# Attention output layer: weight blocks split a block sooner, and the next stage's first two blocks held behind the turned probabilities of heads 5 and 6

## The chip, the cores and the metric

The kernel runs on one core of one Trainium2 chip. The metric is the device time of one execution in microseconds (us), as a median over runs. The kernel before takes 922.94 us (three runs, 922.83 to 923.55). A profiled execution gives the trace from which every time below is read.

## What is computed

A two-layer encoder trunk over 256 rows of 1024 values. Each layer is half a SwiGLU feed-forward, a mixer, and half a SwiGLU feed-forward; the mixer of the first layer is a convolution, that of the second is attention with compressed queries, keys and values. The change touches that attention and the start of the feed-forward behind it:

```
def mla(h, positions, w_a, g_q, g_kv, w_uq, w_ukv, w_o):
    ...
    for blk in range(seq // Q_BLOCK):
        ...
        s = (q_nope . k_nope + q_rope . k_rope) * scale
        s = jnp.where(mask, s, -inf)
        p = softmax(s)
        outs.append(p @ v)
    return concatenate(outs).reshape(seq, N_HEADS * V_HEAD) @ w_o
...
h = h + mla(...)
h = h + 0.5 * swiglu_ffn(rmsnorm(h, ffn_norm2[i]), ...)
```

There are 8 heads, 256 query rows in two blocks of 128, and head widths of 128 (plain), 64 (rotary) and 128 (values).

## The kernel before

**Weights.** All weights stream from HBM in blocks of 128 x 2048 fp32 (1 MB), in one fixed list. `load` (L153) sends a block through three steps: SyncE starts a transfer into a `raw` buffer, ScalarE rounds it into `hi` (L171, two casts of 128 x 1024), VectorE forms the rest `lo = raw - hi` (L175, two subtractions). Four `raw` and four `hi`/`lo` buffers rotate, so a transfer waits for the `lo` of four blocks earlier, and a cast waits until TensorE has read the block four places earlier. A product with weights is three matmuls (`mm3`, L281): `lo` by the high part of the data, `hi` by the high part, `hi` by the low part (L284, L287, L288).

**How far ahead.** `weights(n, more, ahead)` takes the next block of the list and, through `load_ahead`, issues loads for blocks that lie up to `ahead` places on; the default is 2 blocks, `W_BUFS - 1` is 3 and `W_BUFS` is 4. The casts and subtractions are written into the program where `load` is called. A scheduler then orders each engine's instructions; `@urgent` code (softmax, row sums, splits of the data) gets a higher priority, and `behind` keeps weight splits after the last few urgent instructions of the same engine.

**Attention (`mla_in`, L1076).** The last blocks of the list there are, in order, `wuq[2]`, `wuq[0]`, `wukv[0]` (keys), `wukv[1]` (values), `wuq[1]` (queries of heads 4 to 7), and four blocks `wo0` to `wo3` of the output layer. Behind them come `f0`, `f1`, ... of the last feed-forward. For each head: `scores` (L1192) makes the scores `sc` on TensorE, 12 matmuls; `softmax` takes row maxima on VectorE (`nm`, L1209 and L1210), exponentials on ScalarE (`pr`, L1212), and scales them on VectorE (L1214, L1216). `probs` (L1219) turns the probabilities on TensorE (`tp`, three matmuls on L327) and copies them back on ScalarE (`ptT`, L1222). `values` (L1225) multiplies with the values (`pv`, L1227 and L1228), and rounds the result on ScalarE (`Oh`, L1229) with its rest on VectorE (`Ol`, L1230). `Rows` is the output layer: a block of `wo` serves two heads, and each head gives 12 matmuls into `o`.

**The loop (L1239).** Step `i` takes the scores of head `i`, turns head `i-2`, and multiplies head `i-3`; at `i` of 6 and 8 `o.block` adds two heads to the output, and `o.finish` does the last four and goes over to the feed-forward. PSUM has 4 banks for `o` and other products, 3 shared by `sc` and `tp`, and 1 for `pv`; a score tile can only begin when the exponentials that read the bank before it are done.

Of the kernel before, what the change touches and what calls it, by code (L numbers as in the profile page):

```python
# [19 lines left out]
P = 128  # L20
# [19 lines left out]
W_BUFS = 4  # L40
# [47 lines left out]
def trunk(ctx: ExitStack, tc: tile.TileContext, x, xt, pos, invf, gains, gfin, wdw,  # L88
          f1w13, f1w2, f2w13, f2w2, cw1, cw2, wa, wuq, wukv, wo, out):
    nc = tc.nc  # L90
# [12 lines left out]
    def uid(s):  # L103
        n_uid[0] += 1
        return f"{s}_{n_uid[0]}"
# [4 lines left out]
    def bank(tag, name):  # L110
        return ps.tile([P, 512], F32, tag=tag, name=uid(name), bufs=BANKS[tag])
# [30 lines left out]
    def order(ins, first):  # L142
        tc.add_manual_dep(ins.ins, first.name, mybir.DependencyInfo(
            mybir.DependencyClass.NoSync, mybir.DependencyReason.DATA), reason="order")

    def behind(ins):

        for first in ahead_of.get(ins.ins.engine, [])[-BEHIND:]:
            order(ins, first)

    low_later = []

    def load(src, pieces=1):  # L153
        if isinstance(src, tuple) and src[0] == "fast":
            return load_fast(src[1])
        if isinstance(src, tuple):
            raw = rawp.tile([P, HB], F32, tag="raw", name=uid("raw"))
            nc.sync.dma_start(raw, src[1])
            return raw
        later = len(loaded) in (conv_block[-1], conv_block[-2])  # L160
        n = src.shape[-1]
        raw = rawp.tile([P, HB], F32, tag="raw", name=uid("raw"))
        hi = wp.tile([P, HB], F32R, tag="hi", name=uid("hi"))
        lo = wp.tile([P, HB], F32R, tag="lo", name=uid("lo"))
        if len(loaded) < 7:
            fetch(raw[:, :n], src)
        else:
            nc.sync.dma_start(raw[:, :n], src)
        for i in range(pieces):
            c = slice(i * n // pieces, (i + 1) * n // pieces)  # L170
            behind(nc.scalar.copy(hi[:, c], raw[:, c]))  # L171
            if later:
                low_later.append((lo[:, c], raw[:, c], hi[:, c].bitcast(F32)))
            else:
                behind(nc.vector.tensor_sub(lo[:, c], raw[:, c], hi[:, c].bitcast(F32)))  # L175
        return hi, lo

    def load_fast(src):

        raw = rawp.tile([P, HB], F32, tag="raw", name=uid("raw"))  # L180
        sums = rawp.tile([P, HB], F32, tag="raw", name=uid("sums"))
        nc.sync.dma_start(raw, src)
        v = raw.rearrange("p (b n) -> p b n", n=512)
        t = sums.rearrange("p (b n) -> p b n", n=512)
        behind(nc.gpsimd.tensor_tensor(t[:, 0:2, :], v[:, 0:4:3, :], v[:, 1:2, :].to_broadcast([P, 2, 512]), op=ALU.add))  # L185
        behind(nc.vector.tensor_add(t[:, 2, :], t[:, 0, :], v[:, 3, :]))
        behind(nc.vector.tensor_add(t[:, 3, :], t[:, 2, :], v[:, 2, :]))
        out = []
        for x, cols in ((raw, ((0, 512), (1024, 2048))), (sums, ((0, 1024), (1024, 2048)))):
            hi = wp.tile([P, HB], F32R, tag="hi", name=uid("hi"))  # L190
            lo = wp.tile([P, HB], F32R, tag="lo", name=uid("lo"))
            for c0, c1 in cols:
                behind(nc.scalar.copy(hi[:, c0:c1], x[:, c0:c1]))  # L193
                behind(nc.vector.tensor_sub(lo[:, c0:c1], x[:, c0:c1], hi[:, c0:c1].bitcast(F32)))  # L194
            out.append((hi, lo))
        return out
# [14 lines left out]
    def slots(b):  # L211
        return 2 if isinstance(blocks[b], tuple) and blocks[b][0] == "fast" else 1

    def load_ahead(ahead=W_BUFS - 2):
        b = n_used[0]
        while b < len(blocks) and slots(b) <= ahead:
            ahead -= slots(b)
            b += 1
        load_to(b)

    def load_to(last):
        while len(loaded) < last:
            loaded.append(load(blocks[len(loaded)], PIECES))

    def weights(n=1, more=True, ahead=W_BUFS - 2):
        out = []
        for _ in range(n):
            n_used[0] += 1
            if more:
                load_ahead(ahead)  # L230
            else:
                load_ahead(0)
            out.append(loaded[n_used[0] - 1])
        return out
# [12 lines left out]
    def fetch(to, src):  # L247

        dma = nc.sync.dma_start(to, src)
        if first_dma:  # L250
            order(dma, first_dma[-1].ins)
        first_dma.append(dma)

    fetch(xk[:, :1], xt[:, :1])
    for k in range(KT):
        c = slice(k % 4 * 512, k % 4 * 512 + 512)
# [67 lines left out]
    def transposed(src, q, n, after=(), turned=None):  # L324
        b = bank("B", "tp")
        for j in range(n):
            tp = nc.tensor.transpose(b[:, j * P:(j + 1) * P], src[:, (q + j) * P:(q + j + 1) * P], ident)  # L327
            if turned is not None:
                turned.append(tp)
            for a in after:  # L330
                order(tp, a.ins)
        return b
# [743 lines left out]
    def mla_in(act, X, make_next, cc, sn):  # L1076
# [65 lines left out]
        def nope(part, dst, nk, ch, cl, width, h0, heads):  # L1142

            hi, lo = part
            for i in range(heads[0], heads[1], 2):
                b = bank("A", "nope")
                for e in range(2):
                    for k in range(nk):
                        c = slice(k * width + (i + e) * P, k * width + (i + e + 1) * P)
                        mm3(b[:, e * S:(e + 1) * S], hi[:, c], lo[:, c], ch[:, k, :], cl[:, k, :],  # L1150
                            k == 0, k == nk - 1)
                nc.scalar.copy(dst[:, h0 + i:h0 + i + 2, :], b.rearrange("p (e t) -> p e t", t=S))
# [15 lines left out]
        part, = weights()  # L1168
        nope(part, QN, 4, CQh, CQl, 512, 0, (0, 4))
        for t in range(NT):  # L1170
            b = transposed(kd[t], 0, 1)
# [3 lines left out]
        for tb in range(NT):  # L1175
            b = transposed(qr[tb], 0, 4)
            nc.scalar.copy(QR[:, :, tbs(tb)], b.rearrange("p (j t) -> p j t", t=P))
        kpart, = weights()
        nope(kpart, KN, 2, CKh, CKl, D, 0, (0, H))
        (hi, lo), = weights()  # L1180
        for tb in range(NT):
            for d in range(2):
                b = bank("A", "v")
                for k in range(2):
                    c = slice(k * D + d * 512, k * D + d * 512 + 512)
# [6 lines left out]
        def scores(hd):  # L1192
            b = bank("B", "sc")
            sc = {0: b[:, :P], 1: b[:, P:P + S]}
            for qb in range(NT):
                n = (qb + 1) * P
                nc.tensor.matmul(sc[qb], QN[:, hd, tbs(qb)], KN[:, hd, :n], start=True, stop=False)
                nc.tensor.matmul(sc[qb], QR[:, hd // 2, tbs(qb)], KR[:, hd % 2, :n], start=False, stop=False)
                nc.tensor.matmul(sc[qb][:, n - CHUNK:n], mq, mk, start=False, stop=True)
            return softmax(sc)  # L1200
# [18 lines left out]
        def probs(pr):  # L1219
            b = transposed(pr, 0, 3)  # L1220
            pt = act.tile([P, 3 * P], F32, tag="ptT", name=uid("ptT"), bufs=2)
            nc.scalar.copy(pt, b[:, :3 * P])  # L1222
            return pt

        def values(hd, pt):  # L1225
            b = bank("C", "pv")
            nc.tensor.matmul(b[:, :S], VV[:, 0, hd * VH:(hd + 1) * VH], pt[:, :S], start=True, stop=False)  # L1227
            nc.tensor.matmul(b[:, P:S], VV[:, 1, hd * VH:(hd + 1) * VH], pt[:, S:], start=False, stop=True)  # L1228
            nc.scalar.copy(Oh[:, hd, :], b[:, :S])  # L1229
            nc.vector.tensor_sub(Ol[:, hd, :], b[:, :S], Oh[:, hd, :].bitcast(F32))  # L1230

        pr, pt = {}, {}
        pr[0] = scores(0)
        part, = weights()
        nope(part, QN, 4, CQh, CQl, 512, 4, (0, 2))
        pr[1] = scores(1)
        nope(part, QN, 4, CQh, CQl, 512, 4, (2, 4))
        o = Rows(Oh, Ol, H)
        for i in range(2, H + 3):  # L1239
            if i < H:  # L1240
                pr[i] = scores(i)
            if i - 2 < H:
                pt[i - 2] = probs(pr[i - 2])
            if i - 3 in pt:
                values(i - 3, pt[i - 3])
            if i in (6, 8):
                o.block((i - 6) // 2)
        return o.finish(make_next, act)


# [107 lines left out]
def build(shapes):  # L1358
    import concourse.bacc as _bacc

    nc = _bacc.Bacc("TRN2", target_bir_lowering=False, num_devices=1, dynamic_dma_scratch_size=1024)
    args = [nc.dram_tensor(f"in_{n}", s, mybir.dt.from_np(np.dtype(d)), kind="ExternalInput").ap()
            for n, s, d in shapes]
    out = nc.dram_tensor("out", (S, D), F32, kind="ExternalOutput").ap()
    with tile.TileContext(nc, schedule_with_timeline_sim=True) as tc:
        trunk(tc, *args, out)
    return nc
# [9 lines left out]
```

## Time and profile before

| | |
|---|---|
| median of the runs | 922.94 us (922.83 to 923.55) |
| the profiled execution | 923.62 us, of which the span of the trace is 921.8 us |
| TensorE matmul (PE) busy | 909.6 us |
| VectorE (DVE) busy | 680.9 us |
| ScalarE (ACT) busy | 539.7 us |
| GpSimd (POOL) busy | 226.4 us |
| granted TensorE clock | 0.999 |
| the heads' part of attention | about 684 to 734 us from the span's start |

Rows of the timeline read: start, duration, engine, line, operation, out<-in, shapes, count of merged instructions, and in brackets the idle time before and who ended it. Start to start is what one instruction costs its engine; a matmul's duration includes a drain that overlaps the next one.

### The profile page before, as it was taken

Reading aid. Unit: us, or ns where it says so; the run is one execution under the profiler, and the core shown is the slowest. Engines: PE = TensorE matmul, PEld = TensorE weight load, DVE = VectorE, ACT = ScalarE, POOL = GpSimd, SP = SyncE. Lnnn points to the kernel's source line nnn. Section 1 sums busy time; section 2 is a strip of 40 time slices with the busy share of each in tenths; the row PEclk is TensorE's granted clock in tenths of the full one; section 3 lists DMA queues with packets and bytes.
Section 4 is the critical chain, followed back from the end, with each engine's and each line's share of the span. In section 5 each row is a group of like instructions: output and inputs, shape, how many; then the busy total and the mean of one; then the engine's idle time right before and its main releaser. Section 6 shows DMA issues by size and latency. Waiting matters only on the chain.

```text
span 921.8 us, 12383 instructions
## 1 busy us (share of the span) xinstructions
PE 909.6 (99%) x4293; PEld 755.5 (82%) x4293; DVE 680.9 (74%) x1052; ACT 539.7 (59%) x940; POOL 226.4 (25%) x337
## 2 busy tenths in 40 slices
PE   9999999999999999999999999999999999999997
PEld 6888888898958888888888888888998788888886
DVE  5776877689977666777976667978667476667876
ACT  6964556568877455455474544655666475444643
POOL 1101232379941100232300003224200000013223
PEclk9999999999999999999999999999999999999999
DMA  9976656653307676556756775656441557774651
GB/s 342 350 276 226 203 180 222 240 183 138 138 22 283 244 255 240 189 161 228 299 205 238 252 244 153 228 209 214 183 183 60 186 202 251 246 239 150 219 183 47
DMA packets 60399, 191.58 MB, mean 208 GB/s; under 512 B 11184, under 2 KB 33328, under 8 KB 40752
## 3 DMA queue, kind: packets, MB, share of 16 engines
q1 hardware_dynamic: 59760, 190.09, 58.9%
q8 instruction: 34, 0.56, 0.2%
q10 hardware_dynamic: 576, 0.69, 0.2%
q14 instruction: 29, 0.24, 0.1%
HBM read 178.17 MB, written 12.58 MB: 207 GB/s over the span
## 4 chain that ended last, share of the span: by engine, by line
PE 72%; DVE 8%; DMA 8%; ACT 4%; issue 3%; POOL 3%; SPq 1%; POOLq 0%; ACTq 0%; DVEq 0%
PE u L288 15%; PE u L287 15%; PE u L284 15%; DVE lo L175 5%; PE o L284 3%; PE o L287 3%; PE o L288 3%; PE gate L738 3%; DMA raw<-in_f2w 3%; DMA raw<-in_f1w 3%; PE u L738 3%; POOL sums L185 3%; PE o L978 2%; ACT hi L171 1%; DVE lo L194 1%
## 5 line engine op out<-in xcount | busy, mean ns | idle before, releaser
L175 DVE TENSOR_TENSOR lo<-raw,hi 128x1024 fp32r<-128x1024 f32 (+1 forms) x246 | 296.3, 1240 | 74.4 <-ACT hi L171 74.1
L171 ACT CAST hi<-raw 128x1024 fp32r<-128x1024 f32 (+1 forms) x250 | 247.9, 1046 | 147.7 <-PE u L288 107.9
L288 PE MATMUL u<-hi,Xl 128*128 128x512 f32 x688 | 267.8, 390 | 0.7 <-DVE Xl L345 0.7
L284 PE MATMUL u<-lo,Xh 128*128 128x512 f32 x688 | 268.1, 390 | 0.1
L287 PE MATMUL u<-hi,Xh 128*128 128x512 f32 x688 | 267.7, 389 | 0.0
L288 PEld LDWEIGHTS u<-hi,Xl 128*128 128x128 f32 x688 | 129.1, 188 | 28.2 <-DVE Xl L345 1.6
L284 PEld LDWEIGHTS u<-lo,Xh 128*128 128x128 f32 x688 | 129.2, 188 | 27.3 <-DVE lo L175 0.5
L287 PEld LDWEIGHTS u<-hi,Xh 128*128 128x128 f32 x688 | 129.2, 188 | 26.6
L185 POOL TENSOR_TENSOR sums<-raw 128x1024 f32<-128x1024 f32 x20 | 54.2, 2710 | 162.4 <-DMA raw<-in_f2w 52.7
L284 PE MATMUL o<-lo,Gh 128*128 128x512 f32 (+1 forms) x236 | 91.5, 388 | 0.7 <-DVE lo L175 0.7
L287 PE MATMUL o<-hi,Gh 128*128 128x512 f32 (+1 forms) x236 | 91.0, 386 | 0.0
L288 PE MATMUL o<-hi,Gl 128*128 128x512 f32 (+1 forms) x236 | 91.0, 386 | 0.0
L632 POOL TENSOR_TENSOR sx<-gb 128x128 f32<-128x128 f32 x20 | 10.2, 509 | 316.7 <-DMA gb<-gd 316.7
L624 ACT CAST Gh<-gb 128x512 fp32r<-128x512 f32 (+2 forms) x48 | 25.8, 539 | 63.6 <-DMA gb<-gd 63.5
L193 ACT CAST hi<-sums 128x1024 fp32r<-128x1024 f32 x40 | 41.2, 1052 | 30.7 <-PE u L288 14.7
L786 DVE SCALAR_TENSOR_TENSOR acc<-V,dw,acc 128x128 f32<-128x128 f32 (+1 forms) x174 | 57.8, 411 | 0.0
L625 DVE TENSOR_TENSOR Gl<-gb,Gh 128x512 fp32r<-128x512 f32 (+2 forms) x48 | 33.2, 705 | 31.2 <-ACT Gh L624 31.1
L194 DVE TENSOR_TENSOR lo<-sums,hi 128x1024 fp32r<-128x1024 f32 x40 | 56.1, 1432 | 0.0
L284 PEld LDWEIGHTS o<-lo,Gh 128*128 128x128 f32 x236 | 44.3, 188 | 11.0 <-DVE lo L175 2.3
L288 PEld LDWEIGHTS o<-hi,Gl 128*128 128x128 f32 x236 | 44.3, 188 | 8.9
L287 PEld LDWEIGHTS o<-hi,Gh 128*128 128x128 f32 x236 | 44.3, 188 | 8.8
L814 ACT ACTIVATE prod<-V,dw 128x128 f32<-128x128 f32 (+1 forms) x129 | 48.0, 418 | 2.8 <-POOL Y L815 1.4
(247 smaller groups left out, 1325.7 us busy)
## 6 DMA issues: line engine op xcount, KB each, us to landing
raw<-in_f2w SPq DMA_DIRECT2D x66, 1024.0 KB, 4.8
raw<-in_f1w SPq DMA_DIRECT2D x64, 1024.0 KB, 5.0
raw<-in_cw SPq DMA_DIRECT2D x12, 1024.0 KB, 5.2
gd<-gt SPq DMA_DIRECT2D x160, 64.0 KB, 2.7
gb<-gd SPq DMA_DIRECT2D x40, 256.0 KB, 3.4
raw<-in_wo SPq DMA_DIRECT2D x4, 1024.0 KB, 4.8
raw<-in_wuq SPq DMA_DIRECT2D x3, 1024.0 KB, 4.8
raw<-in_f1w SPq DMA_DIRECT2D x8, 256.0 KB, 6.2
```

Of the source, the lines that this page charges most:

```text
L171: behind(nc.scalar.copy(hi[:, c], raw[:, c]))
L175: behind(nc.vector.tensor_sub(lo[:, c], raw[:, c], hi[:, c].bitcast(F32)))
L185: behind(nc.gpsimd.tensor_tensor(t[:, 0:2, :], v[:, 0:4:3, :], v[:, 1:2, :].to_broadcast([P, 2, 512]), op=ALU.add))
L193: behind(nc.scalar.copy(hi[:, c0:c1], x[:, c0:c1]))
L194: behind(nc.vector.tensor_sub(lo[:, c0:c1], x[:, c0:c1], hi[:, c0:c1].bitcast(F32)))
L284: mm = nc.tensor.matmul(o, ah, bl, start=start, stop=False)
L287: nc.tensor.matmul(o, ah, bh, start=False, stop=False)
L288: return nc.tensor.matmul(o, al, bh, start=False, stop=stop)
L625: nc.vector.tensor_sub(dl, x, dh.bitcast(F32))
L738: mm = nc.tensor.matmul(u[:, t], w[:, c], X.x[:, k, t], start=(k == 0), stop=(k == KT - 1))
L786: ins = nc.vector.scalar_tensor_tensor(out if j == j1 - 1 else y, v, w, y, op0=ALU.mult, op1=ALU.add)
L814: prod = nc.scalar.activation(p, v, AF.Copy, scale=w)
```

## The change

The blocks of the output layer are taken one place further ahead (3 instead of 2 at two places, 4 at step `i` = 4), so that `wo0` to `wo3` are all issued before the loop's fourth step. The first two blocks of the feed-forward, `f0` and `f1`, are issued at `i` of 7 and 8, with each cast ordered behind the copy of the turned probabilities of that step (heads 5 and 6). `probs` returns that copy as well.

```
+    split_behind = []
...
-            behind(nc.scalar.copy(hi[:, c], raw[:, c]))
+            high = nc.scalar.copy(hi[:, c], raw[:, c])
+            behind(high)
+            for first in split_behind:
+                order(high, first.ins)
...
-        (hi, lo), = weights()
+        (hi, lo), = weights(1, True, W_BUFS - 1)
...
-            nc.scalar.copy(pt, b[:, :3 * P])
-            return pt
+            return pt, nc.scalar.copy(pt, b[:, :3 * P])
...
-        part, = weights()
+        part, = weights(1, True, W_BUFS - 1)
...
         for i in range(2, H + 3):
+            if i == 4:
+                load_ahead(W_BUFS)
...
-                pt[i - 2] = probs(pr[i - 2])
+                pt[i - 2], last = probs(pr[i - 2])
...
+            if i in (7, 8):
+                split_behind.append(last)
+                load_ahead(W_BUFS)
+                split_behind.clear()
```

No instruction is added or removed on any engine; SyncE and GpSimd keep their order. Line numbers after the change are 2 to 5 higher. Three places show what moves.

**ScalarE, the copies of keys and values before the heads.** `hi_1060` is `wo1`, `KN` the keys (the last copy is that of heads 6 and 7), `VV` the values. Before:

```order
L1152 COPY KN_6043<-nope_1053_6210 128x512
L1152 COPY KN_6043<-nope_1054_6224 128x512
L1152 COPY KN_6043<-nope_1055_6238 128x512
L1187 COPY VV_6045<-v_1059_6260 128x512
L1187 COPY VV_6045<-v_1060_6268 128x512
```

After:

```order
L1157 COPY KN_6043<-nope_1053_6210 128x512
L1157 COPY KN_6043<-nope_1054_6224 128x512
L173 CAST hi_1060_6261<-raw_1059_6260 128x1024 x2
L1157 COPY KN_6043<-nope_1055_6238 128x512
L1192 COPY VV_6045<-v_1062_6268 128x512
L1192 COPY VV_6045<-v_1063_6276 128x512
```

The two casts of `wo1` now stand ahead of the last copy of the keys; the casts of `wo2` take the place, behind the exponentials of head 0, where those of `wo1` stood.

**ScalarE, among the heads.** Before, from the exponentials of head 6 (`pr_1110`) to those of head 7 (`pr_1123`); `hi_1115` and `hi_1118` are `wo2` and `wo3`, `pv_1106` is head 2, `ptT_1112` head 4:

```order
L1212 ACTIVATE pr_1110_6514,sm_1109_6513<-sc_1107_6505,nm_1108_6512 128x256
L171 CAST hi_1115_6535<-raw_1114_6534 128x1024 x2
L171 CAST hi_1118_6543<-raw_1117_6542 128x1024 x2
L1229 CAST Oh_6292<-pv_1106_6500 128x256
L1222 COPY ptT_1112_6527<-tp_1111_6523 128x384
L1212 ACTIVATE pr_1123_6583,sm_1122_6582<-sc_1120_6574,nm_1121_6581 128x128
```

After, the same stretch from head 6 (`pr_1116`) to head 7 (`pr_1123`), with `Oh` of head 2 and `ptT` of head 4:

```order
L1217 ACTIVATE pr_1116_6530,sm_1115_6529<-sc_1113_6521,nm_1114_6528 128x128
L1217 ACTIVATE pr_1116_6530,sm_1115_6529<-sc_1113_6521,nm_1114_6528 128x256
L1233 CAST Oh_6300<-pv_1112_6516 128x256
L1227 COPY ptT_1118_6543<-tp_1117_6539 128x384
L1217 ACTIVATE pr_1123_6583,sm_1122_6582<-sc_1120_6574,nm_1121_6581 128x128
```

No cast of weights is left in it. Those of `wo3` (`hi_1097`) are found after, some ten rows earlier, behind the exponentials of head 3 (`pr_1092`) and ahead of `ptT` of head 2 and the exponentials of head 4 (`pr_1102`):

```order
L1217 ACTIVATE pr_1092_6435,sm_1091_6434<-sc_1089_6426,nm_1090_6433 128x256
L173 CAST hi_1097_6456<-raw_1096_6455 128x1024 x2
L1227 COPY ptT_1104_6485<-tp_1103_6481 128x384
L1217 ACTIVATE pr_1102_6472,sm_1101_6471<-sc_1099_6463,nm_1100_6470 128x128
L1217 ACTIVATE pr_1102_6472,sm_1101_6471<-sc_1099_6463,nm_1100_6470 128x256
L1233 CAST Oh_6300<-pv_1105_6487 128x256
```

So the four casts in one row behind head 6 are gone from there, and two of them stand behind head 3. The casts of `f0` go from behind the exponentials of head 7 to behind `ptT` of head 5; those of `f1` stay behind `ptT` of head 6.

**VectorE, heads 0 to 2.** Before (`nm_1064`, `nm_1072`, `nm_1081` are heads 0, 1, 2; `lo_1069` is `wo1`):

```order
L1209 TENSOR_REDUCE nm_1072_6353<-sc_1071_6346 128x1 x2
L1214 RECIPROCAL sm_1065_6302<-sm_1065_6302 128x2
L1210 TENSOR_SCALAR nm_1072_6353<-nm_1072_6353 128x2
L1216 TENSOR_SCALAR pr_1066_6303<-pr_1066_6303,sm_1065_6302 128x128
L1216 TENSOR_SCALAR pr_1066_6303<-pr_1066_6303,sm_1065_6302 128x256
L175 TENSOR_TENSOR lo_1069_6314<-raw_1067_6312,hi_1068_6313 128x1024 x2
L1214 RECIPROCAL sm_1073_6354<-sm_1073_6354 128x2
```

After (`nm_1067`, `nm_1075` are heads 0 and 1; `lo_1072` is `wo2`):

```order
L1219 RECIPROCAL sm_1068_6310<-sm_1068_6310 128x2
L1214 TENSOR_REDUCE nm_1075_6361<-sc_1074_6354 128x1 x2
L1221 TENSOR_SCALAR pr_1069_6311<-pr_1069_6311,sm_1068_6310 128x128
L1221 TENSOR_SCALAR pr_1069_6311<-pr_1069_6311,sm_1068_6310 128x256
L1215 TENSOR_SCALAR nm_1075_6361<-nm_1075_6361 128x2
L180 TENSOR_TENSOR lo_1072_6322<-raw_1070_6320,hi_1071_6321 128x1024 x2
L1219 RECIPROCAL sm_1076_6362<-sm_1076_6362 128x2
```

The maxima of head 1 have gone behind the reciprocal of head 0, which waits for ScalarE.

## The prediction

> **What bounds the kernel now.** I read the page first, then who waits for whom on PE, then the timelines of PE, ACT and DVE through the heads of attention.
>
> ```profile
> PE 909.6 (99%) x4293; PEld 755.5 (82%) x4293; DVE 680.9 (74%) x1052; ACT 539.7 (59%) x940; POOL 226.4 (25%) x337
> ```
>
> PE bounds the kernel: it is busy for 99% of the span. No instruction is added or taken away, so the time can only move where PE waits. The waits of PE from 695 us on are three groups, of which the first lies in the part that the change touches:
>
> ```profile
> PE o L284 <- ACT Oh L1229: 1.3, 2, 0.9
> PE u L288 <- DVE Xl L345: 0.4, 1, 0.4
> PE o L284 <- DVE lo L175: 0.2, 1, 0.2
> ```
>
> Stage by stage (columns: length, busy time of PE, PEld, DVE, ACT, POOL):
>
> ```profile
> 695.00:722.00 27.00, 25.62 (x146) 21.13 (x144) 18.29 (x51) 16.05 (x43) 0.00 (x0) 1.00 0.37 130
> 722.00:735.00 13.00, 13.00 (x61) 10.61 (x59) 4.20 (x7) 3.51 (x7) 0.00 (x0) 1.00 0.36 136
> ```
>
> PE has 1.38 us of idle time between 695 and 722, and none from there to 735. Ahead of 722 the timeline of PE shows where (a start to a start is the cost; transposes `tp` cost 0.36 from 695.12 to 695.48 when nothing waits):
>
> ```profile
> 695.12 0.53 PE L327 MATMUL tp<-ident,pr 128*128 128x128 f32 x3
> 695.48 0.39 PE L1197 MATMUL sc<-KN,QN 128*128 128x128 f32 x2
> ...
> 711.87 0.53 PE L327 MATMUL tp<-ident,pr 128*128 128x128 f32 x3
> 712.75 0.50 PE L284 MATMUL o<-lo,Oh 128*128 128x512 f32 x1 [0.36 <-ACT Oh L1229]
> ...
> 714.68 0.49 PE L327 MATMUL tp<-ident,pr 128*128 128x128 f32 x3
> 715.27 0.67 PE L1227 MATMUL pv<-ptT,VV 128*128 128x256 f32 x2
> ...
> 716.92 0.61 PE L327 MATMUL tp<-ident,pr 128*128 128x128 f32 x3
> 718.46 0.50 PE L284 MATMUL o<-lo,Oh 128*128 128x512 f32 x1 [0.93 <-ACT Oh L1229]
> ...
> 721.98 0.39 PE L284 MATMUL o<-lo,Oh 128*128 128x512 f32 x1
> ```
>
> Three times the step behind the transposes is late: 0.88 - 0.36 = 0.52, 0.59 - 0.36 = 0.23, and 1.54 - 0.36 = 1.18 us, **1.93 us in all**. (By the Trainium skill, Perfetto Trace Analysis, on the Tensor Engine's instructions, a matmul's end is estimated and not observed. By the idle times in brackets alone the three waits would be 0.36 + 0.93 = 1.29 us and the second would not exist, and the sum below would come to 1.03 us; the starts are why I take 1.93.)
>
> What they wait for stands on ACT and DVE:
>
> ```profile
> 707.74 0.37 ACT L1212 ACTIVATE pr<-sc,nm 128x128 f32<-128x128 f32 x1 [2.30 <-DVE nm L1210]
> 708.55 3.88 ACT L171 CAST hi<-raw 128x1024 fp32r<-128x1024 f32 x4
> 712.33 0.37 ACT L1229 CAST Oh<-pv 128x256 fp32r<-128x256 f32 x1
> 716.15 1.98 ACT L171 CAST hi<-raw 128x1024 fp32r<-128x1024 f32 x2
> 718.04 0.37 ACT L1229 CAST Oh<-pv 128x256 fp32r<-128x256 f32 x1
> ...
> 709.63 3.50 DVE L175 TENSOR_TENSOR lo<-raw,hi 128x1024 fp32r<-128x1024 f32 x3 [0.19 <-ACT hi L171]
> 713.57 1.21 DVE L175 TENSOR_TENSOR lo<-raw,hi 128x1024 fp32r<-128x1024 f32 x1
> 714.71 0.41 DVE L1230 TENSOR_TENSOR Ol<-pv,Oh 128x256 fp32r<-128x256 f32 x1
> ```
>
> `Oh` of head 2 stands behind the four casts of `wo2` and `wo3` (until 712.33), `Ol` of that head, for which the next `pv` waits, behind four subtractions (until 714.71), and `Oh` of head 3 behind the two casts of `f0` (until 718.04). Each wait of PE ends with one of these.
>
> **What the change takes away.** In the new order ACT has no cast between the exponentials of heads 6 and 7, and `f0` stands behind `Oh` of head 3 and `ptT` of head 5. So all three waits lose their cause: -1.93 us, if nothing else is late.
>
> **What it moves.** The casts of `wo1` go ahead of the last copy of the keys, at about 678.9, when that product is done:
>
> ```profile
> 677.87 1.57 ACT L1152 COPY KN<-nope 128x512 f32<-128x512 f32 x3
> 682.84 0.59 ACT L1187 COPY VV<-v 128x512 f32<-128x512 f32 x1 [0.77 <-PE v L288]
> ```
>
> Two casts cost half of 712.33 - 708.55, 1.89 us. The last keys are then copied by 681.3, the first two value products by 682.3, and the third is ready for ACT at 682.8 as before: ACT had idle time ahead of each of them (0.77 us at the third), which hides the casts. PE asks for that keys' copy (its bank) only after the third value product, at about 683. Cost nothing; without that cover up to 1.89 us.
>
> `wo2` takes `wo1`'s old place behind head 0, instruction for instruction. But on DVE the maxima of head 1 now stand behind the reciprocal of head 0, which waits for ACT:
>
> ```profile
> 690.92 0.62 DVE L1209 TENSOR_REDUCE nm<-sc 128x1 f32<-128x128 f32 x2 [0.82 <-PE sc L1199]
> 692.31 0.17 DVE L1214 RECIPROCAL sm<-sm 128x2 f32<-128x2 f32 x1 [0.76 <-ACT pr L1212]
> 693.25 2.36 DVE L175 TENSOR_TENSOR lo<-raw,hi 128x1024 fp32r<-128x1024 f32 x2 [0.19 <-ACT hi L171]
> 696.18 0.62 DVE L1209 TENSOR_REDUCE nm<-sc 128x1 f32<-128x128 f32 x2
> ...
> 697.03 0.37 ACT L1212 ACTIVATE pr<-sc,nm 128x128 f32<-128x128 f32 x1 [0.87 <-DVE nm L1210]
> ...
> 698.00 0.49 PE L1197 MATMUL sc<-KN,QN 128*128 128x128 f32 x2
> ```
>
> Before, the maxima ran at 690.92 while DVE was free. After: reciprocal at 692.31, maxima from 692.39 (0.53 start to start, as 713.04 to 713.57), scales from 692.92 (0.47), the small product 0.12, and the subtractions start at 693.51, not 693.25. All behind them on DVE is 0.26 late: maxima of head 2, its exponentials (697.29), and the scores of head 4 on PE, which need the bank that those exponentials read and start at 698.00 just as they end. **A new wait of 0.26 us**, bounded by nothing (if DVE catches up) and by the 0.62 of the maxima. I take 0.26, from the rows nearest to it. (The Trainium skill, TensorE: Matmul & The Clock Gate, on engine queue depths, calls the queues of ACT and DVE strictly first in, first out. By that rule the maxima cannot pass the waiting reciprocal and the sum is -1.67; were it otherwise it would be -1.93. The trace agrees: `Oh` at 712.33 sat behind four casts.)
>
> The rows of PE's pace and of a set of maxima on DVE:
>
> ```profile
> 696.93 0.52 PE L327 MATMUL tp<-ident,pr 128*128 128x128 f32 x3
> ...
> 720.41 0.59 PE L1227 MATMUL pv<-ptT,VV 128*128 128x256 f32 x2
> ...
> 720.98 1.17 PE L288 MATMUL o<-hi,Ol 128*128 128x512 f32 x4
> ...
> 713.04 0.61 DVE L1209 TENSOR_REDUCE nm<-sc 128x1 f32<-128x128 f32 x2
> ```
>
> `wo3`'s casts go behind the exponentials of head 3, about 700.3 to 702.2, ahead of `ptT` of head 2 and the exponentials of head 4, and DVE's first subtraction ahead of head 4's `nm`. This is the place where a new wait could arise, so I walk it, with 0.81 us for a set of exponentials (707.74 to 708.55), 1.14 for a subtraction (713.57 to 714.71) and PE's own pace from 695.12: 1.45 us a score tile (695.48 to 696.93), 0.36 transposes, 0.57 a `pv` (720.41 to 720.98), 0.25 an `o` matmul (four from 720.98 to 721.98). DVE: behind the reciprocal of head 2 at 698.3 come the maxima of head 3 and the scales of head 2, so `nm` of head 3 is done at 699.5 and its exponentials end at 700.4; behind scales and maxima the first subtraction starts at 701.7, `nm` of head 4 is done at 703.0, the exponentials of head 4 at 704.0. PE needs them for the scores of head 6, after the transposes of head 2 (699.7), eight `o` matmuls, `pv` of head 1 (702.0), the scores of head 5 (703.1) and the transposes of head 3 (705.1): at **705.5, a margin of 1.4 us**. `ptT` of head 2, due at 707.7, is done at 702.7. Further on the margins grow: `Oh` of head 2 is done at 709.5 and asked for at 712.7, `Oh` of head 3 at 714.8 and asked for at 716.5. The tightest is at the transposes of head 2: scales done at 699.4, asked for at 699.7. Each hand-off costs a microsecond of PE per microsecond late once its margin is gone.
>
> The transfers of `f1` and later blocks go out earlier, since the subtractions that free their buffers do; SyncE keeps its order, and no PE wait in this stage is on a transfer. Worth nothing.
>
> **What follows behind.** From 722 to 735 PE is busy throughout, and its order there is the same, so the gain passes. In the last feed-forward the chain leaves PE once, at 853.7, and comes back at 894.28 through subtractions, transfers and GpSimd:
>
> ```profile
> 853.71 0.13 PE u L288
> 853.86 2.09 DVE lo L175 x2
> ...
> 894.28 0.50 PE o L284
> ```
>
> It starts from a PE matmul, so it moves as a whole. Sum: -1.93 + 0.26 = **-1.67 us**. The profiled execution took 923.62 us (0.68 above the median, with the same instructions), which would become 921.95; off the median, 922.94 - 1.67 = **921.3 us**, 0.18% faster. A change under 0.2% (1.85 us) is about what a measurement of this kernel cannot tell from none, and the forecast lies just inside that line.
>
> **Rivals.**
> *The new wait does not arise, or the last stage closes its own.* DVE could make up the 0.26 us if its small steps overlap more than their rows show; the wait at 894.28 (0.23) could go if a transfer is quicker. Then -1.93 to -2.2: 920.7 to 921.0. Against it: from 693.25 on DVE's rows follow each other without idle time.
>
> *A wait is left.* The margins hang on pace; were the tight one at the transposes of head 2, or `Oh` of head 3, missed, some 0.5 to 1 us comes back: 921.8 to 922.3.
>
> *It does not do what it says.* `f1` keeps its place in ACT's order, and holding it changes nothing; if the casts of `wo3` merely make the same waits two heads sooner, the gain is given back: 922.9. The margin of 1.4 us speaks against it.
>
> *Slower: ACT's queue stands still for `wo1`.* Its casts now stand ahead of the last keys' copy and all four value copies, so a late transfer stops ACT, then PE at the fourth value product.
>
> ```profile
> 669.38 0.33 SPq L168 DMA_DIRECT2D raw<-in_wo  x1
> ...
> DMA to landing us min/median/max: 4.6/4.8/5.9
> ```
>
> Issued at 669.38, it lands at about 674.2, and the casts come at 678.9: 4.7 us of slack, and 1.7 more until PE asks. It decides from a transfer of 11.2 us on, a microsecond for each beyond, and passes 922.94 by 0.2% at 14.7 us (924.8). The longest transfer around there took 5.9.
>
> **How the numbers follow.** The forecast has a chance of 0.62; the runs of before lie 0.72 us apart, so about a third of it (0.20) comes out past the 0.2% line and 0.42 within. The first rival has 0.26 (0.25 faster, 0.01 within), a wait left 0.05, nothing gained 0.03, slower 0.04. Faster 0.45, within 0.51, slower 0.04. The range runs from 920.4 (all waits gone, 0.23 of the last stage too, and 0.4 of scatter) to 922.4 (a microsecond back and some scatter); slower and no gain are left out.
>
> **What would show it.** In the new profile PE should have no wait on `Oh` between 700 and 722, PE's starts behind the transposes of heads 5, 6 and 7 should follow at 0.36, the subtractions of `wo2` should start about 0.26 later than `wo1`'s did, and the scores of head 4 should start 0.26 later. The first `o` matmul of `wo2` should stand at about 720.3 in place of 721.98, and all later stages be shorter by nothing. Wrong would be: a wait on `pr` before the scores of head 6, one of `v` on the keys' copy near 683, or an end of the stage that moved without the end of the span.

## The result and the profile after

The changed kernel takes 921.88 us (median of 13 runs), beside 923.71 us for the kernel before in the same runs. The ratio is 0.9978, with a 95% interval of 0.9969 to 0.9987: 2.0 us less, between 1.2 and 2.9. The forecast was 1.67 us less. The profiled execution took 923.03 us, against 923.62 before, and that difference of 0.59 says little by itself, as will be seen.

PE's busy time on the page is 909.6 us, as before. The waits of PE from 695 us on, in the changed kernel:

```profile
PE o L289 <- DVE lo L180: 0.7, 1, 0.7
PE u L293 <- DVE Xl L350: 0.4, 1, 0.4
```

The group of waits on `Oh`, 1.3 us before, is gone. The wait on `lo`, which stands in the last stage, has grown from 0.2 to 0.7.

To compare runs, whose times are already apart when attention begins, I measure one stretch on PE by two rows: the first product behind the transposes of the keys, and the first transpose of `h`. Before the change:

```profile
673.79 0.39 PE L284 MATMUL nope<-CKl,hi 128*128 128x256 f32 x1
...
735.18 0.55 PE L327 MATMUL tp<-ident,h 128*128 128x128 f32 x3
```

After it:

```profile
674.73 0.38 PE L289 MATMUL nope<-CKl,hi 128*128 128x256 f32 x1
...
734.17 1.53 PE L332 MATMUL tp<-ident,h 128*128 128x128 f32 x9
```

The attention part takes 735.18 - 673.79 = 61.39 us before and 734.17 - 674.73 = 59.44 us after: **1.95 us less**. The view by windows says what kind of time went. Its columns are length and busy time of PE, PEld, DVE, ACT and POOL; first before:

```profile
673.79:735.18 61.39, 59.84 (x349) 51.15 (x349) 34.67 (x78) 34.08 (x77) 0.00 (x0) 1.00 0.37 137
```

After:

```profile
674.73:734.17 59.44, 59.21 (x349) 51.13 (x349) 33.92 (x78) 33.72 (x77) 0.00 (x0) 1.00 0.40 142
```

The same 349 matmuls; PE's idle time falls from 1.55 to 0.23 us, and 0.63 us of "busy" time went too: modelled ends had covered part of the waits.

The timeline of PE after the change, at the places that the prediction named (attention begins 0.94 us later in this trace, so I say that its clock, the time scale of the trace, is that much ahead of the one before):

```profile
698.70 0.38 PE L1232 MATMUL pv<-ptT,VV 128*128 128x128 f32 x2
699.15 0.49 PE L1202 MATMUL sc<-KN,QN 128*128 128x128 f32 x2
...
713.09 0.53 PE L332 MATMUL tp<-ident,pr 128*128 128x128 f32 x3
713.37 0.49 PE L289 MATMUL o<-lo,Oh 128*128 128x512 f32 x1
...
715.05 0.49 PE L332 MATMUL tp<-ident,pr 128*128 128x128 f32 x3
715.29 0.72 PE L293 MATMUL o<-hi,Ol 128*128 128x512 f32 x2
...
719.06 0.49 PE L332 MATMUL tp<-ident,pr 128*128 128x128 f32 x3
719.38 0.60 PE L1231 MATMUL pv<-ptT,VV 128*128 128x256 f32 x2
```

Behind the transposes of heads 5, 6 and 7 PE now goes on after 0.28, 0.24 and 0.32 us, where it took 0.88, 0.59 and 1.54. What comes next is not in all three the same matmul as before, since PE's matmuls among the heads stand in another order too. The scores of head 4 start at 699.15 - 0.94 = 698.21 on the old clock, 0.21 late: the new wait. ACT, from the exponentials of head 7 on:

```profile
714.21 0.37 ACT L1217 ACTIVATE pr<-sc,nm 128x128 f32<-128x128 f32 x1 [2.30 <-DVE nm L1215]
...
715.25 0.38 ACT L1233 CAST Oh<-pv 128x256 fp32r<-128x256 f32 x1
...
715.89 2.01 ACT L173 CAST hi<-raw 128x1024 fp32r<-128x1024 f32 x2
```

`Oh` of head 3 now runs ahead of the casts of `f0`, and the exponentials of head 7 start 2.02 us sooner on the old clock (715.29 before, 714.21 - 0.94 = 713.27 after).

### The profile page after: what moved, and what is told of

It is laid out like the page before. It is cut to its first block, busy times and chain, and to the rows that moved or that the text cites. A ratio compares the mean times of both kernels' runs of the same rounds, so it can differ in the third digit from the quotient of the medians.

```text
span 921.2 us, 12383 instructions
## 1 busy us (share of the span) xinstructions
PE 909.6 (99%) x4293; PEld 755.9 (82%) x4293; DVE 680.9 (74%) x1052; ACT 539.0 (59%) x940; POOL 227.4 (25%) x337
## 4 chain that ended last, share of the span: by engine, by line
PE 80%; DVE 6%; DMA 4%; ACT 4%; issue 3%; POOL 2%; SPq 0%; POOLq 0%; DVEq 0%; ACTq 0%
PE u L293 16%; PE u L289 16%; PE u L292 16%; PE o L289 5%; PE o L292 5%; PE o L293 5%; DVE lo L180 3%; PE gate L743 3%; PE u L743 3%; DMA raw<-in_f1w 2%; POOL sums L190 2%; PE o L983 2%; DMA raw<-in_f2w 1%; ACT hi L173 1%; PE p L289 1%
```

## The experiments

Each trace is read by three lengths on PE: the attention part as above, its beginning (to the first scores of head 4), and the last stage (from the first transpose of `h` to the matmul behind PE's last wait, 894.28 before). Ratios are to the kernel before, run beside each.

| kernel | attention | to scores of head 4 | last stage | median us | ratio, 95% interval |
|---|---|---|---|---|---|
| before | 61.39 | 24.21 | 159.10 | 923.71 | |
| the change | 59.44 | 24.42 | 159.55 | 921.88 | 0.9978 (0.9969 to 0.9987) |
| the change again | 59.45 | 24.44 | 159.36 | 921.62 | 0.9980 (0.9971 to 0.9989) |
| hold of `f0`, `f1` only | 60.10 | 24.22 | 159.30 | 922.48 | 0.9983 (0.9969 to 0.9996) |
| lead of `wo` only | 59.40 | 24.40 | 159.54 | 921.86 | 0.9971 (0.9959 to 0.9983) |
| change, maxima first | 59.20 | 24.24 | 159.67 | 921.07 | 0.9962 (0.9949 to 0.9975) |
| lead of `wo1` only | 59.02 | 24.20 | 159.16 | 920.99 | 0.9960 (0.9946 to 0.9973) |
| the same again | 59.05 | 24.22 | 159.99 | 920.28 | 0.9964 (0.9949 to 0.9979) |
| lead of `wo1`, `wo2` only | 59.41 | 24.44 | 159.13 | 921.45 | 0.9979 (0.9970 to 0.9988) |
| casts held, no lead | 59.23 | 24.21 | 159.66 | 921.15 | 0.9975 (0.9965 to 0.9984) |

My theory was that each wait of PE belongs to the casts that stand ahead of one `Oh` or `Ol`, and that the new wait is made by DVE's order. The rivals: the earlier lead itself brings the gain, or ACT's casts make the new wait.

**The hold of `f0` and `f1` alone.** Against the change:

```
-        (hi, lo), = weights(1, True, W_BUFS - 1)
+        (hi, lo), = weights()
...
-        part, = weights(1, True, W_BUFS - 1)
+        part, = weights()
...
-            if i == 4:
-                load_ahead(W_BUFS)
```

> Only the hold of the feed-forward's first two blocks behind the turned probabilities; the blocks of the output layer keep their old lead, so the four casts of wo2 and wo3 still stand behind the exponentials of head 6, ahead of Oh of head 2. The attention part is measured on PE from the first product behind the transposes of the keys (673.79 before, 674.73 after) to the first transpose of h (735.18, 734.17): 61.39 us before, 59.44 after. Theory (each wait belongs to the casts that stand ahead of one Oh or Ol): only the third wait goes, worth 1.2, and no new wait comes: 60.2 us, the waits ahead of Oh and Ol of head 2 stay at 0.5 and 0.25 in the trace, the time 1.2 us under that of before. Rival (the gain comes from the earlier lead of the output layer's blocks and their transfers): nothing gained here, 61.4 us.

Measured: 60.10 us. ACT and PE of this kernel:

```profile
708.53 3.88 ACT L173 CAST hi<-raw 128x1024 fp32r<-128x1024 f32 x4
712.31 0.37 ACT L1233 CAST Oh<-pv 128x256 fp32r<-128x256 f32 x1
...
716.17 0.37 ACT L1233 CAST Oh<-pv 128x256 fp32r<-128x256 f32 x1
...
716.81 2.01 ACT L173 CAST hi<-raw 128x1024 fp32r<-128x1024 f32 x2
```

```profile
712.73 0.53 PE L289 MATMUL o<-lo,Oh 128*128 128x512 f32 x1 [0.36 <-ACT Oh L1233]
...
714.72 0.49 PE L332 MATMUL tp<-ident,pr 128*128 128x128 f32 x3
715.25 0.67 PE L1231 MATMUL pv<-ptT,VV 128*128 128x256 f32 x2
...
716.90 0.40 PE L289 MATMUL o<-lo,Oh 128*128 128x512 f32 x1
```

The four casts and the first two waits are where they were; the third wait is gone, for 1.29 us. The theory holds here.

**The lead of the output layer's blocks alone.** Against the change:

```
-            if i in (7, 8):
-                split_behind.append(last)
-                load_ahead(W_BUFS)
-                split_behind.clear()
```

> Only the earlier lead of the output layer's blocks; the feed-forward's blocks are not held, and the casts of the first one stand again ahead of Oh of head 3 and behind the exponentials of head 7. Theory: the first two waits go (0.9 with their restarts), the new one of 0.2 at the scores of head 4 stays, the third stays at 1.0 to 1.5: 60.4 to 60.9 us for the attention part (before 61.39, after 59.44), the time 0.5 to 1.0 us under that of before. Rival (the hold is only a safeguard, the lead alone brings the gain): 59.4 us as in the change.

Measured: 59.40 us, the whole gain. My expectation failed: the casts of `f0` do stand ahead of `Oh` of head 3 again, and PE does not wait. ACT and PE:

```profile
713.58 0.37 ACT L1217 ACTIVATE pr<-sc,nm 128x128 f32<-128x128 f32 x1 [2.30 <-DVE nm L1215]
...
714.39 1.99 ACT L173 CAST hi<-raw 128x1024 fp32r<-128x1024 f32 x2
716.28 0.37 ACT L1233 CAST Oh<-pv 128x256 fp32r<-128x256 f32 x1
```

```profile
716.57 0.49 PE L332 MATMUL tp<-ident,pr 128*128 128x128 f32 x3
716.82 0.48 PE L289 MATMUL o<-lo,Oh 128*128 128x512 f32 x1
```

The exponentials of head 7 start at 713.58 instead of 715.29 (2.04 us sooner, with this clock 0.33 ahead), because DVE's maxima of head 7 no longer stand between the subtractions of `wo2` and `wo3`. They start as soon as PE has the scores:

```profile
712.66 0.62 DVE L1214 TENSOR_REDUCE nm<-sc 128x1 f32<-128x128 f32 x2 [2.00 <-PE sc L1204]
```

So the casts of `f0` let `Oh` of head 3 begin at 716.28. It is done at 716.65, 0.17 us before PE takes it at 716.82: a small margin. The third wait needed both: the late exponentials and the casts of `f0` behind them. Either taken away removes it, and the hold adds nothing to the lead.

**The change with the maxima of head 1 ahead of head 0's reciprocal on DVE.** Against the change (`top` is the last `reduce_max` of the head):

```
+            recips.append(nc.vector.reciprocal(sm, sm))
+            if len(recips) == 2:
+                order(recips[0], top.ins)
```

> The change, with the reciprocal of head 0 put behind the maxima of head 1 on DVE, as it stood before the change. Theory (the new wait of 0.2 at the scores of head 4 is made by that order on DVE): that wait goes, 59.2 us for the attention part (after 59.44), 0.2 us less than the change, below what the timed runs can tell. Rival (the wait is made on ACT by the casts of wo2 ahead of the exponentials of head 1): still there, 59.4 us.

Measured: 59.20 us, 0.24 less, and the beginning back from 24.42 to 24.24. DVE of this kernel (its clock is 1.42 behind the one before):

```profile
689.53 0.62 DVE L1216 TENSOR_REDUCE nm<-sc 128x1 f32<-128x128 f32 x2 [1.30 <-PE sc L1204]
690.91 0.17 DVE L1221 RECIPROCAL sm<-sm 128x2 f32<-128x2 f32 x1 [0.76 <-ACT pr L1219]
...
691.85 2.36 DVE L180 TENSOR_TENSOR lo<-raw,hi 128x1024 fp32r<-128x1024 f32 x2 [0.19 <-ACT hi L173]
```

Against the same rows of the change itself:

```profile
693.27 0.17 DVE L1219 RECIPROCAL sm<-sm 128x2 f32<-128x2 f32 x1 [2.68 <-ACT pr L1217]
693.35 0.60 DVE L1214 TENSOR_REDUCE nm<-sc 128x1 f32<-128x128 f32 x2
...
694.33 0.16 DVE L1215 TENSOR_SCALAR nm<-nm 128x2 f32<-128x2 f32 x1
694.40 2.35 DVE L180 TENSOR_TENSOR lo<-raw,hi 128x1024 fp32r<-128x1024 f32 x2
```

In the change the maxima wait behind a reciprocal that itself waited 2.68 us, and the subtractions start 694.40 - 693.27 = 1.13 us behind it, with the maxima first 691.85 - 690.91 = 0.94. The casts of `wo2` on ACT stand in the same place in both kernels, so they did not make the wait.

**The lead of `wo1` alone.** Against the kernel before, one line that has an effect (the lines for the hold are there, with nothing to hold behind):

```
-        (hi, lo), = weights()
+        (hi, lo), = weights(1, True, W_BUFS - 1)
```

> Of the whole change one line: the block of the values is taken with a lead of 3, so that wo1 is split a block sooner; neither wo2 and wo3 nor the feed-forward's blocks are treated otherwise than before. The scheduler then puts Oh of head 2 ahead of the exponentials of head 6 and so ahead of the four casts of wo2 and wo3, and Oh of head 3 and the turned probabilities of head 5 ahead of the feed-forward's casts; wo2 is not between the exponentials of heads 0 and 1. Theory (only what stands ahead of Oh and Ol of heads 2 and 3 counts, and DVE's late maxima make the new wait): all three waits go and no new one comes, 59.2 us for the attention part, 2.2 us under before, no worse than the whole change. Rival (the four casts in one row stop ACT whatever stands ahead of them): a wait of about 1 us at the turned probabilities of head 4, Oh of head 3 or the transposes of head 7, 60.2 us or more.

Measured: 59.02 us, and 59.05 in a second run, the shortest of all. ACT:

```profile
705.88 0.37 ACT L1233 CAST Oh<-pv 128x256 fp32r<-128x256 f32 x1 [1.00 <-PE pv L1232]
...
706.97 3.88 ACT L173 CAST hi<-raw 128x1024 fp32r<-128x1024 f32 x4
...
711.29 0.37 ACT L1233 CAST Oh<-pv 128x256 fp32r<-128x256 f32 x1
...
714.45 1.99 ACT L173 CAST hi<-raw 128x1024 fp32r<-128x1024 f32 x2
```

The four casts still stand in one row of 3.88 us. But `Oh` of head 2 stands ahead of them and `Oh` of head 3 ahead of those of `f0`, and PE waits for neither. DVE still takes the maxima of head 1 behind the reciprocal, yet the beginning is 24.20: without subtractions of `wo2` behind them, the lateness reaches nobody. And the casts of `wo1` ahead of the last copy of the keys cost nothing.

The second run of this kernel:

> The version with one line of the change once more, beside the change on one chip: 59.0 us again for the attention part, 0.4 us under the change, which the timed runs cannot tell apart with certainty; if the wo2 and wo3 loads made the loss in the last stage, 159.1 to 159.2 there again, and then some 0.9 us under the change.

Measured: 59.05 us for the attention part, as expected, but 159.99 in the last stage. So a loss there comes without the earlier loads of `wo2` and `wo3` too.

**The lead of `wo1` and `wo2`, without `wo3`'s step and without the hold.** Against the change, the lines of `i == 4` and of `i in (7, 8)` are left out.

> The lead of 3 for the blocks of the values and of the last queries (wo1 and wo2 a block sooner), but neither wo3 at step 4 nor the hold. Oh of heads 2 and 3 stand ahead of the casts that they waited for, and the subtractions of wo2 stand between the maxima of heads 1 and 2 as in the change. Theory (those subtractions behind the late maxima make the new wait): the three waits gone, the new one of 0.2 at the scores of head 4 there: 59.2 to 59.4 us for the attention part, 0.2 to 0.4 above the version with wo1 alone. Rival (the scheduler's order of TensorE decides, not the waits): somewhere else, 59.0 or above 59.6.

Measured: 59.41 us, with a beginning of 24.44. The new wait comes with the subtractions of `wo2` at that place. The two steps left out bring nothing: without them the part is 0.03 us shorter, as much as two runs of one kernel differ.

**The casts held, and no lead.** Against the kernel before (`values` returns the cast of `Oh`, kept in `rounded`, and `load` orders its casts behind `split_behind` as in the change):

```
+            if i == 6:
+                split_behind.append(rounded[2])
             if i in (6, 8):
                 o.block((i - 6) // 2)
+            split_behind.clear()
```

> The kernel before with one edit: at step 6 the casts of wo2 and wo3 are held behind Oh of head 2; no load is issued sooner. Theory (a wait is paid by who stands ahead in the queues, not by how early a block is split): the first two waits go, and the third too, since Oh of head 3 then stands ahead of the feed-forward's casts; but the maxima of head 7 still stand between the subtractions on DVE, so its exponentials and with them the transposes of head 7 may be late by up to 1.5: 59.3 to 60.8 us for the attention part. Rival (the earlier lead is what counts): 61.4 us as before.

Measured: 59.23 us. ACT:

```profile
708.71 0.38 ACT L1233 CAST Oh<-pv 128x256 fp32r<-128x256 f32 x1 [0.35 <-PE pv L1232]
...
709.35 3.90 ACT L173 CAST hi<-raw 128x1024 fp32r<-128x1024 f32 x4
713.62 0.37 ACT L1233 CAST Oh<-pv 128x256 fp32r<-128x256 f32 x1 [0.37 <-PE pv L1232]
...
715.71 0.37 ACT L1217 ACTIVATE pr<-sc,nm 128x128 f32<-128x128 f32 x1 [1.34 <-DVE nm L1215]
...
716.51 1.99 ACT L173 CAST hi<-raw 128x1024 fp32r<-128x1024 f32 x2
```

All three waits are gone with no block split sooner: for these waits, who stands ahead in the queue is what counts, not the lead. The exponentials of head 7 are even later than before (715.71, with this clock 0.34 behind, against 715.29), and the wait that I thought possible at the transposes of head 7 does not come: these transposes stand later on PE too, at 719.12 and not at 716.92 as before, behind matmuls on `Oh` of head 3 (with the hold alone they are at 718.73). PE's order by itself would not have removed the third wait, since `Oh` of head 3 began only at 718.04 before the change.

**The change once more.**

> The changed kernel once more, beside the others on one chip. The attention part should be 59.4 us again. From the first transpose of h to the first matmul behind the last wait of PE the traces so far show 159.11 (before), 159.55 (the change), 159.30, 159.54, 159.67 and 159.16 (the experiments), so the change lost 0.44 of its 1.95 there in its trace. If that loss is the change's own, it is 159.5 to 159.6 again; if it is scatter of the last stage's small transfers, it may be anything between 159.1 and 159.7.

Measured: 59.45 us and 159.36. The last stage of one and the same kernel lay at 159.55 and 159.36 here, and at 159.16 and 159.99 in the two runs with the lead of `wo1`: it scatters by 0.8 us, and what the change's trace lost there is within that. PE's last wait in that trace of the change:

```profile
893.72 0.50 PE L289 MATMUL o<-lo,Gh 128*128 128x512 f32 x1 [0.67 <-DVE lo L180]
```

## Why the prediction came out nearly right, point by point

- **The three waits.** Gone, as forecast, but they were worth more. From the scores of head 4 to the first transpose of `h` it is 735.18 - 698.00 = 37.18 us before and 734.17 - 699.15 = 35.02 after: 2.16, not 1.93. The failed step is the price of transposes when nothing waits. I took 0.36 from 695.12, where scores stand before and behind them. Between scores and an `o` they cost 0.28 (713.09 to 713.37), between an `o` and `pv` 0.32 (719.06 to 719.38), between two `o` 0.25 (716.57 to 716.82, with the lead of `wo` only). With these the waits are 0.88 - 0.28, 0.59 - 0.32 and 1.54 - 0.25, or 2.16, and the third alone is the 1.29 that the hold of `f0` removed. It is not only what follows that sets the price. Scores follow here too, and it is 0.32, behind an `o` (trace of the change):

```profile
705.47 0.70 PE L293 MATMUL o<-hi,Ol 128*128 128x512 f32 x2
706.02 0.49 PE L332 MATMUL tp<-ident,pr 128*128 128x128 f32 x3
706.34 0.39 PE L1202 MATMUL sc<-KN,QN 128*128 128x128 f32 x2
```

- **Starts against bracketed idle times.** The starts were right: by the idle times alone 1.29 us would have gone.
- **What the third wait hung on.** I gave it to the casts of `f0` by themselves, and so its removal to the hold. Both halves were wrong as a rule: the lead alone removes it, by way of DVE, the maxima and the exponentials of head 7, and the hold removes it as well. The sum was not touched, since the change does both.
- **The new wait.** 0.21 us (24.42 - 24.21) against a forecast of 0.26, at the place named, and by the order on DVE: 0.18 of it goes when that order is undone (24.24). The small product ahead of the subtractions took 0.07 (694.33 to 694.40) where I had put 0.12. (The Trainium skill, TensorE: Matmul & The Clock Gate, on engine queue depths, has ACT and DVE strictly first in, first out. The trace agrees: maxima that could have run earlier started at 693.35, right behind a reciprocal that had waited 2.68 us.)
- **`wo1` ahead of the keys.** Nothing, as forecast: the beginning of the run with this move alone is 24.20. The slower rival did not come up.
- **`wo3` behind head 3.** The walk gave a margin of 1.4 us at the scores of head 6. The exponentials of head 4 end at 704.68 in the trace of the change, and those scores start at 706.34. No wait arose there or at the transposes of head 2.
- **What follows behind.** The gain passes, but not in each single trace. In the change's trace 0.45 was lost in the last stage, and 0.94 before attention began. The latter lies on instructions that the change does not touch: 0.92 of it is there at the first transposes of `h` on PE (278.05 before, 278.97 after). In the second trace of the change attention began at 672.72, not at 674.73. So 1.95 - 0.94 - 0.45 = 0.56 of the two spans' difference of 0.6 is explained, and the ratio over the timed runs, where such scatter should even out, shows 2.0.

So the forecast of -1.67 is -1.93 + 0.26, and the runs show -2.16 + 0.21 = -1.95. Both terms erred the same way, so the errors did not cancel. At 0.9978 the ratio lies just past the line of 0.2% that the forecast lay inside.

**A better version** is the lead of `wo1` alone: 59.02 us for the attention part, 0.42 under the change. It takes away a fourth wait, which the kernel before has already. I had read the scores of head 4 as starting at 698.00 just as the exponentials end, and put no wait there. PE before the change:

```profile
697.73 0.38 PE L1228 MATMUL pv<-ptT,VV 128*128 128x128 f32 x2
698.00 0.49 PE L1197 MATMUL sc<-KN,QN 128*128 128x128 f32 x2
698.32 0.39 PE L1198 MATMUL sc<-KR,QR 128*128 128x128 f32 x2
```

With the lead of `wo1` alone (its clock is 1.28 behind):

```profile
696.48 0.38 PE L1232 MATMUL pv<-ptT,VV 128*128 128x128 f32 x2
696.71 0.39 PE L1202 MATMUL sc<-KN,QN 128*128 128x128 f32 x2
696.93 0.39 PE L1203 MATMUL sc<-KR,QR 128*128 128x128 f32 x2
```

The two steps take 0.27 and 0.32 us before, 0.45 and 0.32 in the change, 0.23 and 0.22 here. That is 0.32 of the 0.42; the other 0.10 is not traced. The exponentials of head 2, for which these scores wait, start 0.81 us sooner than before (694.94 here, 697.03 before), since no subtractions of weights stand ahead of that head's maxima on DVE. The change kept this wait and made it longer.

The version's times are 0.9960 and 0.9964 of before, 3.3 to 3.7 us, which is more than the 2.37 of its attention part. The intervals reach down to 1.9 us, so scatter may be the reason. That it is faster than the change by more than 0.42 stays open.

## What to carry to other kernels

When an engine with a queue in order feeds the one that bounds, look for what stands ahead of the small instruction that is waited for. Moving the one behind the other (59.23 us with an ordering alone, 59.02 with one line of lead) gave at least as much as splitting three blocks sooner and holding two (59.44). Price a wait from start to start against the same hand-off without a wait, with the same kind of matmul on either side. Compare kernels over the stretch that the edit touches: it repeated within 0.03 us, while the rest of the span differed by 2.0 and 2.7 us between two runs of one kernel, more than the gain.

## What was not expected of the hardware

- A set of three transposes of the probabilities holds PE for 0.24 to 0.36 us, and both neighbours count. Behind scores it costs 0.36 ahead of scores or `pv` and 0.28 ahead of an `o`. Behind an `o` or `pv` it costs 0.32 and 0.24. All the traces agree within 0.01 where nothing waits.
- The same program reached attention at 672.51 and 674.36 (lead of `wo1` only) or at 672.72 and 674.73 (the change), and its last stage took 159.16 and 159.99, or 159.55 and 159.36. Stretches far from the edit vary by 0.2 to 2.0 us between executions. The runs do not show why.
